# New places for the pieces of a head's step in a gated delta layer, and for a pair of query blocks in sparse attention

## The chip, the cores and the metric

The kernel runs on one core of a Trainium2 chip. The time is the device time of one execution in microseconds (us); a kernel's time is the median of several executions. A profile is one further execution, recorded instruction by instruction.

## The reference, cut to what matters

Two layers over 2048 tokens of width 1024: sparse attention on a shared latent (8 heads, 256 selected keys a query), then a gated delta layer (8 heads of 128, causal convolution, decay, a state carried over the sequence). Each is followed by its output projection and a gated embedding.

```
def sparse_latent_attention(q_lat, q_idx, w_idx, c_kv, k_idx, rel_bias, topk):
    ...
        _, sel = lax.top_k(score, topk)
        ...
        logits = jnp.einsum("bqhc,bqkc->bqhk", qb, c_sel).astype(jnp.float32)
        logits = logits + jnp.moveaxis(bias, -1, 2).astype(jnp.float32)
        logits = jnp.where(valid[:, :, None, :], logits, NEG_INF)
        prob = jax.nn.softmax(logits, axis=-1).astype(c_sel.dtype)
        return jnp.einsum("bqhk,bqkc->bqhc", prob, c_sel)

def chunked_gated_delta_rule(q, k, v, g, beta):
    ...
    lower = jnp.where(strict, jnp.einsum("bhntd,bhnjd->bhntj", kb, kc) * decay, 0.0)
    a_mat = lower + jnp.eye(CHUNK, dtype=jnp.float32)
    rhs = jnp.concatenate([vc * bc[..., None], kb * jnp.exp(gc)[..., None]], axis=-1)
    sol = lax.linalg.triangular_solve(a_mat, rhs, left_side=True, lower=True)
    u_pre, w_dec = sol[..., :dv], sol[..., dv:]
    aqk = jnp.where(incl, jnp.einsum("bhntd,bhnjd->bhntj", qc, kc) * decay, 0.0)
    ...
    def step(state, xs):
        u_p, w_d, a_qk, q_d, k_d, cd = xs
        u = u_p - jnp.einsum("bhck,bhkv->bhcv", w_d, state)
        o = jnp.einsum("bhck,bhkv->bhcv", q_d, state) + jnp.einsum("bhct,bhtv->bhcv", a_qk, u)
        state = state * cd[..., None, None] + jnp.einsum("bhck,bhcv->bhkv", k_d, u)
        return state, o
```

## The kernel before

The program runs in five stages, one after the other: projections, index scores and top-k (`phase1`), attention (`phase2`), the first output projection with its gate (`mix(0)`), the delta layer (`phase4`), and the second output projection (`mix(1)`). Matmuls take f32 values as a high and a low part (three matmuls for one product, `mm3_step`, lines 90 to 92).

Inside a stage several generators run side by side. Each yields a number, its place, ahead of each piece of work, and `weave` always resumes the one with the lowest place. The order in which the pieces are recorded is a priority: a scheduler then orders each engine's instructions by it, with its own estimate of when each is ready, so that an engine's order differs a little from the recorded one. The numbers in the program therefore set what stands behind what on TensorE (PE), VectorE (DVE), ScalarE (ACT), GpSimd (POOL) and in the DMA queue of SyncE (SP). Every engine runs its own list in order.

*Attention.* A piece is a pair of query blocks g (0 to 7) of a head h. `at_logits` computes the pair's logits (`lg`, with penalties added into `pr` by DVE, then Exp on ACT); `at_values` transposes the probabilities (`turn`: `pt`, split by ACT and DVE into `ph` and `pl`) and multiplies them with the values (`mult`: `po`). `cost` gives a pair's length in units, `begin` its place, `DELTA` the lag of values behind logits, `MP` the place of `mult` within a step of `turn`, and `at_loads` places the loads of the next pairs.

*The delta layer.* `phase4` goes through 16 steps j (8 heads for each half of the sequence) and two more at the end. In step j these run side by side:

- `project(j)`: the projections k, q, z, v of head j: 4 x 2 x 24 = 192 matmuls of 128x512 (`pBk`, `pBq`, `pBz`, `pBv`, L1521 to L1523), each result then copied by ACT and convolved by DVE (taps, L1466). The next weights are loaded (L1310) and split by `raw_weights` into `wB`: high part on ACT (L1317), low part on DVE (L1319).
- `within(j-1)`: the inverse of the chunk's triangular matrix: transposes `pkt`, products `pkk`, 16 pairs of product and sum on DVE (`tmp`, `inv`, L1639 and L1642), a round trip of `inv` through DRAM (L1648, L1649), its transposition `Tc` (L1652), and from `LV` on the small matmuls `px`, `pd`, `px_1`, `pd_2` that assemble the inverse `U`.
- `beside(j-1)`: `pqs`, `pkq` and the transposes `pvt`.
- `across(j-2)`: the state through 8 chunks c, one after the other: `pks` (PE) to `y` (DVE, L1749) to `pu` (PE) to `uu` (ACT) to `po` (PE) to `state` (DVE, L1762) to the next `pks`. Chunk c has the place `AC + c * AD`.
- `gated(j-3)`: the output of a finished head: `pot`, and the gate.

At the end `ahead` splits the next stage's weights (`wo`, ACT with DVE or POOL) and begins its first products (`poe`).

Of the kernel before, what the change touches and what calls it, by code (L numbers as in the profile page):

```python
# [27 lines left out]
NC = 8  # L28
# [10 lines left out]
def tile_trunk(ctx: ExitStack, tc: tile.TileContext, a: dict, out: bass.AP):  # L39
# [152 lines left out]
    def enter(sb, xbufs):  # L192

        xs = [load_x(sb, b) for b in range(xbufs - 1)]
        hT = None
        for b in range(4):
            for i in range(2):
                yield i / 8 + b / 4
                if hT is None:

                    n = KD if st1["early"] else 2
                    hT = [T(*(("hT", 2) if st1["early"] else ("c8", 4)), [P, n, 2, SB], f"hT{next(uid)}", F32R)
                          for _ in range(0, KD, n)]
                    st1["hT", sb] = [hT[k // n][:, k % n] for k in range(KD)]
                if i == 0 and b + xbufs - 1 < 4:
                    xs.append(load_x(sb, b + xbufs - 1))
                pt = ps("pp", 4, f"xT{sb}_{b}_{i}")
                for k in range(4):
                    nc.tensor.transpose(pt[:, k * P:(k + 1) * P], xs[b][:, (i * 4 + k) * P:(i * 4 + k + 1) * P], ident)
                ts_ = slice(b * P, (b + 1) * P)  # L210
                m = min(n, 4)
                for k in range(i * 4, i * 4 + 4, m):
                    h = hT[k // n][:, k % n:k % n + m]
                    split(pt[:, (k - i * 4) * P:(k - i * 4 + m) * P].rearrange("p (k n) -> p k n", k=m),
                          h[:, :, 0, ts_], h[:, :, 1, ts_])
# [375 lines left out]
    def phase1():  # L591
        with scope("keys", True) as keys:
# [22 lines left out]
            with scope("scores") as base:  # L615
# [13 lines left out]
                def rest():  # L629

                    work = WORK
                    place, t, done = [(0, 0.0)], 0, 0.0
                    while t < total:
                        t += 1
                        done += 1 - sum(w / (b - a_) for sb, w in work.items() for a_, b in [index_at[sb]] if a_ < t <= b)
                        place.append((t, done))

                    def when(w):
                        w = w / whole * place[-1][1]
                        while place and place[0][1] < w and len(place) > 1:  # L640
                            place.pop(0)
                        return place[0][0]

                    parts = [([gates_z(sb) for sb in range(NSB)], 44), ([proj_q()], WQ),
                             ([proj_k(), *([proj_v1()] if VB else [])], WK)]
                    parts = [parts["zqk".index(c)] for c in RO]
                    whole = sum(len(g) * w for g, w in parts)
                    w0 = 0
                    with scope("rest"):
                        for gens, w in parts:  # L650
                            for g in gens:
                                for f in g:
                                    yield when(w0 + f * w)
                                w0 += w
# [254 lines left out]
    PRL, PRS, AHEAD = 4, 4, 2  # L909
    C0, DELTA = 1.5, 7  # L910

# [12 lines left out]
    def phase2():  # L924
# [155 lines left out]

        cost = [4 * g + 3 + C0 for _, g in order]
        begin = list(itertools.accumulate([0] + cost))
# [33 lines left out]
        def at_loads():  # L1116
# [7 lines left out]
            penalties(range(4, 8))  # L1124
            yield -VS + VL * 0.52
            coming[2]()
# [3 lines left out]
            for n, (h, g) in enumerate(order):  # L1130
                yield begin[max(n - 2, 0)] - 0.02
                if n >= 2:
                    prepare(h, g)
                if n % 8 == 3:
                    coming = fetch(h + 1)
                if n >= 3:
                    f = next(coming, None)
                    if f:
                        f()
# [232 lines left out]

    VT, RA, RB = 0.36, 0.31, 0.0127
    AC, AD, LV = 0, 0.11, 0.75
    FX = 0.02

    def phase4():
# [92 lines left out]
        def project(j):  # L1470
# [12 lines left out]
            for i, name in enumerate("kqzv"):  # L1483
# [7 lines left out]
                for sb in range(2):  # L1491
                    ss_ = slice(sb * SB, (sb + 1) * SB)
                    pp = ps("pa", 2, f"pB{name}{j}_{sb}")
                    for k in range(KD):
# [13 lines left out]
                        if new and sb == 1 and k == 7:  # L1508
                            for _ in e:
                                yield at  # L1510
                        if i == GI and sb == 1 and k == 2:
                            gb = m["gb"] = T("raw", 3, [P, NC, P], f"gb{j}", where=pre)
                            g = gc_d[half]
                            nc.sync.dma_start(gb, bass.AP(g.tensor, g.offset + h * P, [[0, P], [H * P, NC], [1, P]]))
                        if n + 1 < 64 and n % 32 != 31:
                            if sb == 0 and k == 0:
                                made["raw"] = load_weights(n + 1)
                            elif sb == 1 and k == 0:
                                ready[n + 1] = raw_weights(n + 1, made.pop("raw"))
# [16 lines left out]

        def by4(name, mm, sink, at):

            for g in range(2):
                yield at  # L1540
                pp = ps("g", 3, f"{name}_{g}")
# [11 lines left out]
        def within(j):  # L1553
# [41 lines left out]

            yield from by4(f"pkk{j}", prod(kT, kT), l_sink, 0.06)
            if j - 2 in ended:
# [70 lines left out]
            for p in range(2):  # L1668
                e, o = q[2 * p], q[2 * p + 1]
                yield LV + 0.06 + p * 0.02  # L1670
                pd = ps("g", 3, f"pd{j}_{p}")
# [21 lines left out]
        def beside(j):  # L1693

            m = made[j]
            yield 0.12
            kT, qT, vT, kt, nk, dT = (m[x] for x in "k q v kt nk dT".split())
# [32 lines left out]
        def across(j):  # L1730
# [7 lines left out]
            for c in range(NC):  # L1738
                first = half == 0 and c == 0
                t0 = AC + c * AD  # L1740
                y = T("gy", 6, [P, P], f"y{j}_{c}")
# [3 lines left out]
                else:  # L1745
# [6 lines left out]
                    nc.scalar.activation(qs, p1[:, P:2 * P], AF.Copy, scale=eg[:, c, h:h + 1])  # L1752
                yield t0 + 0.035
                p2 = ps("r", 3, f"pu{j}_{c}")
                nc.tensor.matmul(p2[:, 0:P], U[:, c], y, start=True, stop=True)
                uu = T("gy", 6, [P, P], f"uu{j}_{c}")
                last["ACT"] = nc.scalar.activation(uu, p2[:, 0:P], AF.Copy, scale=cj[:, c:c + 1]).ins
                yield t0 + 0.07
                p3 = ps("r", 3, f"po{j}_{c}")
# [39 lines left out]
        def ahead(part):  # L1799

            if part == 0:
                for r in range(8):
                    yield r / 16
                    wout(1, r)
            n = (2, EARLY - 2)[part]
            for x in range(n):
                b = len(early)
                at = 0.5 + x * 0.25 if part == 0 else x / n
                yield at
# [3 lines left out]
                for c in range(2):  # L1813
                    cs = slice(c * 512, (c + 1) * 512)
                    pp = ps("pa", 2, f"poe{b}_{c}")
                    for k in range(KD):
                        t = wo[1][k // 4][:, k % 4, :, cs]
                        mm3_step(pp, y[:, 0, k], y[:, 1, k], t[:, 0], t[:, 1], k == 0, k == KD - 1)
                        if k % 2:
                            yield at + (c * 4 + k // 2 + 1) / 9 * (0.25 if part == 0 else 1 / n)  # L1820
                    nc.vector.tensor_tensor(xt[:, cs], pp, xt[:, cs], ALU.add)
# [6 lines left out]
        for j in range(n + 2):  # L1828
# [12 lines left out]
    F1 = 3  # L1841
    MP = 0.9
    VB = 3
    RO = "zkq"
    WQ = 90
    WK = 42
    VS, VL, V0, V1 = (40, 39.5, 39, 20)
    PLAN = ({3: (0, 120), 2: (120, 260), 1: (300, 400), 0: (430, 470)},
            {3: (122, 300), 2: (302, 415), 1: (417, 480), 0: (482, 530)}, 520)
    pre = ctx.enter_context(tc.tile_pool(name="pre", bufs=1))  # L1850
# [74 lines left out]
```

## Time and profile before

| what | us |
|---|---|
| median of 3 runs | 3472.86 (3471.24 to 3486.31) |
| the profiled execution | 3468.28 |
| its span, first to last instruction | 3466.6 |
| attention in it | about 920 to 1440 |
| delta layer in it | about 1860 to 3110 |

In the rows of the profile `pu L1755 <- DVE y L1749` reads: the instruction on `pu` at line 1755 waited for the one on `y` at line 1749. "x8" counts instructions in a row that is merged; a number in brackets is the time that the engine stood idle before it. The granted clock is TensorE's, 1.00 being full.

### The profile page before, as it was taken

To read this page: it belongs to the slowest core of one execution; us is meant where nothing else is said; L and a number is where in the kernel's file an instruction comes from. 1 tells how busy PE (TensorE), PEld (TensorE's weight loads), DVE (VectorE), ACT (ScalarE), POOL (GpSimd) and SP (SyncE) were. 2 spreads that over 40 slices of the span, in tenths; PEclk is the share of its full clock that TensorE was granted. 3 is DMA by queue.
4 is the path that set the end of the run, shared out by engine and by line. 5 is a ranking of instruction groups with operands and counts; after the bars stand their busy time and mean duration, and the time that the engine had idled before them with its cause. 6 is when DMAs were issued, how large, how long until landed. Compare 5 with 4: busy or idle time off the path is not lost.

```text
span 3466.6 us, 52296 instructions
## 1 busy us (share of the span) xinstructions
PE 3321.1 (96%) x19082; PEld 2786.5 (80%) x19082; DVE 2102.7 (61%) x4566; ACT 1882.7 (54%) x3319; POOL 943.2 (27%) x1620
## 2 busy tenths in 40 slices
PE   8999988988899999999999999999999999899999
PEld 6778777877799999888887788887788888778887
DVE  5367896865588888622225667667667676633222
ACT  5366947675677777543335565555555555433221
POOL 2022435145645444211100221222121222321100
PEclk9999998999899999999999999999999999899999
DMA  6322344442522222422223222213222222233211
GB/s 218 114 77 68 102 148 145 172 152 98 183 78 85 80 85 74 136 95 64 72 64 94 58 50 55 53 45 93 54 58 50 58 51 57 86 130 116 73 34 72
DMA packets 325294, 311.71 MB, mean 90 GB/s; under 512 B 69448, under 2 KB 272808, under 8 KB 322984
## 3 DMA queue, kind: packets, MB, share of 16 engines
q1 hardware_dynamic: 325032, 308.33, 29.8%
q8 instruction: 150, 2.46, 0.3%
q14 instruction: 112, 0.92, 0.1%
HBM read 212.85 MB, written 95.42 MB: 89 GB/s over the span
## 4 chain that ended last, share of the span: by engine, by line
PE 53%; DVE 11%; DMA 4%; ACT 2%; POOL 2%; issue 2%; SPq 0%; DVEq 0%; ACTq 0%; POOLq 0%
PE pgm L91 3%; PE pgm L92 3%; PE pgm L90 3%; PE pt L1024 3%; DVE tmp L1639 3%; PE pom L91 2%; PE pom L90 2%; PE pom L92 2%; PE po L1044 2%; PE po L1045 2%; PE pBv L1521 2%; PE pBv L1522 2%; DVE inv L1642 2%; PE lg L92 2%; PE pBv L1523 2%
## 5 line engine op out<-in xcount | busy, mean ns | idle before, releaser
L79 DVE TENSOR_TENSOR pl<-pt,ph 128x512 fp32r<-128x512 f32 (+1 forms) x288 | 187.5, 657 | 45.8 <-ACT ph L78 43.6
L78 ACT ACTIVATE ph<-pt 128x512 fp32r<-128x512 f32 (+1 forms) x288 | 160.1, 564 | 97.5 <-PE pt L1024 90.3
L1006 ACT ACTIVATE pr<-pr,nm,qscale 128x1024 f32<-128x1024 f32 (+2 forms) x192 | 189.6, 988 | 41.0 <-DVE nm L1003 39.7
L423 DVE SCALAR_TENSOR_TENSOR score<-rl,wi,score 128x1024 f32<-128x1024 f32 (+7 forms) x154 | 169.0, 1119 | 39.6 <-ACT rl L415 38.8
L1247 DVE TENSOR_TENSOR gm<-ppm,gm 128x512 f32<-128x512 f32 x64 | 43.4, 689 | 244.4 <-ACT gm L1246 244.4
L1024 PE MATMUL pt<-ident,pr 128*128 128x128 f32 x1088 | 169.6, 276 | 7.6 <-ACT pr L1006 4.9
L729 DVE TENSOR_SCALAR_CACHE_REDUCE tkj<-score,t 128x1664 bf16<-128x1664 f32 (+3 forms) x91 | 121.7, 1353 | 86.8 <-POOL t L769 79.2
L415 ACT ACTIVATE rl<-il 128x1024 f32<-128x1024 f32 (+7 forms) x176 | 143.2, 819 | 54.8 <-PE il L92 49.2
L90 PE MATMUL pom<-wo,ym 128*128 128x512 f32 x432 | 171.0, 396 | 1.9 <-DVE y L1056 1.1
L91 PE MATMUL pom<-wo,ym 128*128 128x512 f32 x432 | 168.9, 391 | 1.3 <-POOL wo L87 1.3
L91 PE MATMUL pgm<-wm,xh 128*128 128x512 f32 x432 | 168.7, 390 | 1.5 <-DVE wm L82 1.5
L90 PE MATMUL pgm<-wm,xh 128*128 128x512 f32 x432 | 168.8, 391 | 0.6 <-ACT gm L1246 0.6
L92 PE MATMUL pom<-wo,ym 128*128 128x512 f32 x432 | 168.8, 391 | 0.0
L92 PE MATMUL pgm<-wm,xl 128*128 128x512 f32 x432 | 168.7, 390 | 0.0
L1044 PE MATMUL po<-pl,kv 128*128 128x256 f32 x576 | 162.8, 283 | 1.2 <-DVE pl L79 1.2
L1043 PE MATMUL po<-ph,kv 128*128 128x256 f32 x576 | 160.9, 279 | 1.5 <-ACT ph L78 1.5
L1045 PE MATMUL po<-ph,kv 128*128 128x256 f32 x576 | 162.1, 281 | 0.0
L87 POOL TENSOR_TENSOR ym<-yr,ym 128x1024 fp32r<-128x1024 f32 x32 | 77.1, 2409 | 303.5 <-ACT ym L86 303.4
L1246 ACT ACTIVATE gm<-pgm,rm_r 128x512 f32<-128x512 f32 x64 | 42.9, 684 | 183.8 <-PE pgm L91 117.5
L87 POOL TENSOR_TENSOR w<-wr,w 128x512 fp32r<-128x512 f32 x74 | 107.0, 1456 | 130.8 <-ACT w L86 122.8
L1752 ACT ACTIVATE qs<-pks,eg 128x128 f32<-128x128 f32 x120 | 44.0, 367 | 177.5 <-DVE y L1749 171.1
L727 ACT ACTIVATE tkj<-score,t 128x1920 bf16<-128x1920 f32 (+3 forms) x91 | 127.8, 1405 | 23.0 <-POOL t L769 19.8
(636 smaller groups left out, 10908.5 us busy)
## 6 DMA issues: line engine op xcount, KB each, us to landing
wBr<-in_b_w_in_dram SPq DMA_DIRECT2D x64, 512.0 KB
wr<-in_a_w_in_dram SPq DMA_DIRECT2D x74, 256.0 KB
yr<-yT_d SPq DMA_DIRECT2D x32, 512.0 KB
x<-in_x_dram SPq DMA_DIRECT2D x16, 512.0 KB
xn_d<-x SPq DMA_DIRECT2D x16, 512.0 KB
x<-xn_d SPq DMA_DIRECT2D x16, 512.0 KB
zT_d<-z SPq DMA_DIRECT2D x32, 256.0 KB
k_d<-k SPq DMA_DIRECT2D x16, 512.0 KB
```

The source lines that it names most:

```text
L78: nc.scalar.activation(hi, src, AF.Copy)
L79: nc.vector.tensor_tensor(lo, src, f32(hi), ALU.subtract)
L87: nc.gpsimd.tensor_tensor(lo, src, f32(hi), ALU.subtract)
L90: nc.tensor.matmul(dst, ah, bh, start=first, stop=False)
L91: nc.tensor.matmul(dst, ah, bl, start=False, stop=False)
L92: nc.tensor.matmul(dst, al, bh, start=False, stop=last)
L423: nc.vector.scalar_tensor_tensor(sc[:, s0:s1], rl[:, :s1 - s0], w, sc[:, s0:s1], ALU.mult, ALU.add)
L1006: nc.scalar.activation(pr[:, s0:s1], pr[:, s0:s1], AF.Exp, bias=nm, scale=sc, accum_out=den[:, i % 2, x:x + 1])
L1024: nc.tensor.transpose(pt[:, x * P:(x + 1) * P], probs[h, i][:, j * P:(j + 1) * P], ident)
L1043: nc.tensor.matmul(d, V[0][:, j], ph[:, c], start=st, stop=False)
L1044: nc.tensor.matmul(d, V[0][:, j], pl[:, c], start=False, stop=False)
L1045: nc.tensor.matmul(d, V[1][:, j], ph[:, c], start=False, stop=sp)
```

## The change

Numbers only, but for one condition: places of pieces in attention and in the delta layer. Every engine has the same instructions as before, in another order, but for two loads of an activation table on ACT that fall away (each is put where two neighbours need different tables). Phase 1 stays as it was (its lines in the diff are other ways of writing the same numbers). The core of the diff:

```
-    C0, DELTA = 1.5, 7
+    C0, DELTA = 1.269, 8.2959
-        cost = [4 * g + 3 + C0 for _, g in order]
+        cost = [3.7993 * g + 3 + C0 for _, g in order]
-            yield -VS + VL * 0.52
+            yield -VS + VL * 0.6127
-                yield begin[max(n - 2, 0)] - 0.02
+                yield begin[max(n - 2, 0)] - 1.0534
-    MP = 0.9
+    MP = 1.3291
...
-    VT, RA, RB = 0.36, 0.31, 0.0127
-    AC, AD, LV = 0, 0.11, 0.75
-    FX = 0.02
+    VT, RA, RB = 0.3282, 0.31, 0.0127
+    AC, AD, LV = 0.0, 0.11, 0.8179
+    FX = 0.0219
...
-                            if sb == 0 and k == 0:
+                            if (sb, k) == (0, 0):
                                 made["raw"] = load_weights(n + 1)
-                            elif sb == 1 and k == 0:
+                            if (sb, k) == (0, 7):
                                 ready[n + 1] = raw_weights(n + 1, made.pop("raw"))
...
-            yield from by4(f"pkk{j}", prod(kT, kT), l_sink, 0.06)
+            yield from by4(f"pkk{j}", prod(kT, kT), l_sink, 0.06, 0.0105)
-            yield 0.12
+            yield 0.086
-                t0 = AC + c * AD
+                t0 = AC + c * AD - (0.0317 if c == NC - 1 else 0)
-                yield t0 + 0.035
+                yield t0 + 0.0279
-                yield t0 + 0.07
+                yield t0 + 0.0918
-                at = 0.5 + x * 0.25 if part == 0 else x / n
+                at = 0.5842 + x * 0.25 if part == 0 else x / n
```

What that does to the engines' lists is shown at three places. The names are those of the program; in `y_6`, `pks_6`, `po_5` the number behind the name is the chunk c.

DVE in the middle of a head's step (step j = 5), before, from the state of chunk 5 to `y` of chunk 6:

```order
L1762 SCALAR_TENSOR_TENSOR state<-state,cd_23341,po_5_24443 128x128
L1639 TENSOR_TENSOR tmp_24083<-inv_24082,blk_24076 128x392
L1766 TENSOR_TENSOR vt_23564<-po_5_24443,qs_5_24415 128x128
L1642 TENSOR_REDUCE inv_24082<-tmp_24083 128x7x2
L1319 TENSOR_TENSOR wB_24449<-wBr_24386,wB_24449 128x1024
L1639 TENSOR_TENSOR tmp_24083<-inv_24082,blk_24076 128x480
L1749 SCALAR_TENSOR_TENSOR y_6_24448<-pks_6_24466,neg_21234,vt_23564 128x128
```

The same place now:

```order
L1319 TENSOR_TENSOR wB_24436<-wBr_24386,wB_24436 128x1024
L1639 TENSOR_TENSOR tmp_24090<-inv_24089,blk_24083 128x364
L1762 SCALAR_TENSOR_TENSOR state<-state,cd_23341,po_5_24454 128x128
L1642 TENSOR_REDUCE inv_24089<-tmp_24090 128x7x2
L1766 TENSOR_TENSOR vt_23564<-po_5_24454,qs_5_24415 128x128
L1639 TENSOR_TENSOR tmp_24090<-inv_24089,blk_24083 128x392
L1749 SCALAR_TENSOR_TENSOR y_6_24459<-pks_6_24466,neg_21234,vt_23564 128x128
```

The split `wB` has moved from between the state and `y_6` to ahead of the state, and the product 128x480 from before `y_6` to behind it.

TensorE near the end of the same step, before: the small matmuls that assemble the inverse, among the last projection (`pBv_1`), behind 172 of the step's 192 projection matmuls:

```order
L1523 MATMUL pBv_1_24609<-hB_0_20698,wB_24449 128x512
L1521 MATMUL pBv_1_24609<-hB_0_20698,wB_24449 128x512
L1664 MATMUL px_00_24512<-Tc_24481,LT_23991 32x32 x8
L1664 MATMUL px_01_24536<-Tc_24481,LT_23991 32x32 x8
L1522 MATMUL pBv_1_24609<-hB_0_20698,wB_24449 128x512
L1523 MATMUL pBv_1_24609<-hB_0_20698,wB_24449 128x512
L1673 MATMUL pd_0_24558<-Uc_24480,X_0_24511 32x32 x8
L1673 MATMUL pd_1_24583<-Uc_24480,X_0_24511 32x32 x8
```

Now, behind 179 of them:

```order
L1521 MATMUL pBv_1_24583<-hB_0_20698,wB_24436 128x512
L1522 MATMUL pBv_1_24583<-hB_0_20698,wB_24436 128x512
L1664 MATMUL px_00_24542<-Tc_24485,LT_23991 32x32 x8
L1664 MATMUL px_01_24557<-Tc_24485,LT_23991 32x32 x8
L1523 MATMUL pBv_1_24583<-hB_0_20698,wB_24436 128x512
L1521 MATMUL pBv_1_24583<-hB_1_20699,wB_24436 128x512
L1673 MATMUL pd_0_24591<-Uc_24484,X_0_24535 32x32 x8
L1673 MATMUL pd_1_24610<-Uc_24484,X_0_24535 32x32 x8
```

The group has moved seven projection matmuls on. Its last member, `pd_2`, had six projection matmuls behind it in the step and now stands at the start of the next step, right ahead of the transposes `pkt`; `pu_0` of that next step stands six projection matmuls earlier than before.

DVE at the end of the layer, when no projection is left, before: `y` of chunk 1 of the last head but one, and what stands around it:

```order
L1577 TENSOR_SCALAR ncj_31734<-cj_31730 128x8
L1775 SCALAR_TENSOR_TENSOR ss_31706<-ss_31706,sq_30561 128x8
L1749 SCALAR_TENSOR_TENSOR y_1_31800<-pks_1_31809,neg_26493,vt_31283 128x128
L1594 SCALAR_TENSOR_TENSOR LT_31705<-pkk_0_31758,ncj_31734,dT_31737 128x128 x4
L1594 SCALAR_TENSOR_TENSOR LT_31705<-pkk_1_31767,ncj_31734,dT_31737 128x128 x4
L1600 RECIPROCAL rs_31707<-rs_31707 128x8
```

Now:

```order
L1766 TENSOR_TENSOR vt_31283<-po_0_31797,qs_0_31712 128x128
L1594 SCALAR_TENSOR_TENSOR LT_31705<-pkk_0_31758,ncj_31734,dT_31737 128x128 x4
L1594 SCALAR_TENSOR_TENSOR LT_31705<-pkk_1_31771,ncj_31734,dT_31737 128x128 x4
L1775 SCALAR_TENSOR_TENSOR ss_31706<-ss_31706,sq_30561 128x8
L1749 SCALAR_TENSOR_TENSOR y_1_31802<-pks_1_31811,neg_26487,vt_31283 128x128
L79 TENSOR_TENSOR wo_4_31869<-wor_4_31870,wo_4_31869 128x1024
```

The eight products `LT` have moved from behind `y_1` to ahead of it.

More of the change, by code (lines that the diff above doesn't have):

```diff
@@ L197, in enter @@
             for i in range(2):
-                yield i / 8 + b / 4
+                yield (i / 8 + b / 4)
                 if hT is None:
@@ L642, in when @@
                         return place[0][0]
-                    parts = [([gates_z(sb) for sb in range(NSB)], 44), ([proj_q()], WQ),
+                    parts = [([gates_z(sb) for sb in range(NSB)], 44.0), ([proj_q()], WQ),
                              ([proj_k(), *([proj_v1()] if VB else [])], WK)]
@@ L1510, in project @@
                                 yield at
-                        if i == GI and sb == 1 and k == 2:
+                        if i == GI and (sb, k) == (1, 2):
                             gb = m["gb"] = T("raw", 3, [P, NC, P], f"gb{j}", where=pre)
@@ L1535, in ch, with by4 @@
             return slice(c * P, (c + 1) * P)
-        def by4(name, mm, sink, at):
+        def by4(name, mm, sink, at, more=0.0):
             for g in range(2):
-                yield at
+                yield at + g * more
                 pp = ps("g", 3, f"{name}_{g}")
@@ L1669, in within @@
                 e, o = q[2 * p], q[2 * p + 1]
-                yield LV + 0.06 + p * 0.02
+                yield LV + 0.0609 + p * 0.02
                 pd = ps("g", 3, f"pd{j}_{p}")
@@ L1802, in ahead @@
                 for r in range(8):
-                    yield r / 16
+                    yield r * 0.0625
                     wout(1, r)
@@ L1819, in ahead @@
                         if k % 2:
-                            yield at + (c * 4 + k // 2 + 1) / 9 * (0.25 if part == 0 else 1 / n)
+                            yield at + (c * 4 + k // 2 + 1) / 9 * (0.25 if part == 0 else 1.3319 / n)
                     nc.vector.tensor_tensor(xt[:, cs], pp, xt[:, cs], ALU.add)
@@ L1841, in tile_trunk @@
     F1 = 3
-    MP = 0.9
+    MP = 1.3291
     VB = 3
     RO = "zkq"
[L1845 to L1849, printed above, removed]
+    WQ = 90.0
+    WK = 42.0
+    VS, VL, V0, V1 = (40.0, 39.3825, 38.628, 20)
+    PLAN = ({3: (0, 120), 2: (120, 260), 1: (300, 400), 0: (430, 470)}, {3: (122, 300), 2: (302, 415), 1: (417, 480), 0: (482, 530)}, 520)
     pre = ctx.enter_context(tc.tile_pool(name="pre", bufs=1))
```

## The prediction

> **What bounds the kernel now.** I read the page first, then the busy time by stretch, the waits of TensorE, the granted clock in short stretches, and at last single rows in order of time.
>
> ```profile
> span 3466.6 us, 52296 instructions
> PE 3321.1 (96%) x19082; PEld 2786.5 (80%) x19082; DVE 2102.7 (61%) x4566; ACT 1882.7 (54%) x3319; POOL 943.2 (27%) x1620
> ```
>
> TensorE is busy 96% of the span, and no instruction is added or dropped on it. All that new places can win is the 145 us in which it stands still, and time lost to a lowered clock. The next rows show how much of it lies where the change reaches: attention (about 920 to 1440 us) and the delta layer (about 1860 to 3110 us).
>
> ```profile
> 920.00:1440.00 520.00, 515.70 (x3780) 483.14 (x3779) 450.25 (x1423) 380.53 (x711) 239.44 (x288) 1.00 0.28 84
> ...
> 1990.00:2300.00 310.00, 304.83 (x1992) 253.25 (x1991) 218.99 (x502) 176.35 (x338) 71.89 (x163) 0.99 0.23 54
> 2300.00:2520.00 220.00, 205.01 (x1329) 165.93 (x1328) 146.25 (x325) 115.63 (x213) 47.30 (x108) 0.96 0.27 68
> 2520.00:2935.00 415.00, 407.69 (x2737) 339.72 (x2736) 292.26 (x661) 235.98 (x450) 100.35 (x228) 1.00 0.23 54
> 2935.00:3110.00 175.00, 160.79 (x952) 128.87 (x951) 94.70 (x214) 75.39 (x145) 50.62 (x66) 0.91 0.31 94
> ```
>
> The columns are busy time of PE, its weight load, DVE, ACT and POOL, then the clock. Attention has 4.3 us of idle PE in 520 us. The quiet heads of the delta layer (1990 to 2300 and 2520 to 2935) have 5.2 and 7.3 us. The turn between the halves of the sequence (2300 to 2520) has 15.0 us at clock 0.96, the end of the layer 14.2 us at clock 0.91. So the delta layer decides. Its waits on TensorE, from 1860 to 3110 us:
>
> ```profile
> PE pu L1755 <- DVE y L1749: 15.0, 16, 3.4
> ...
> PE pks L1747 <- DVE state L1762: 5.5, 6, 2.5
> PE px L1664 <- DVE Tc L1652: 5.3, 3, 2.5
> ...
> PE pBz L1521 <- ACT wB L1317: 1.4, 2, 0.9
> ```
>
> Then the clock (the third number from the end), in stretches that I cut where it falls:
>
> ```profile
> 1960.00:1965.00 5.00, 5.00 (x36) 3.67 (x33) 1.64 (x2) 1.81 (x3) 0.68 (x2) 0.66 0.06 14
> 2245.00:2250.00 5.00, 5.00 (x45) 3.64 (x43) 1.22 (x3) 1.38 (x3) 0.22 (x2) 0.67 0.51 72
> 2315.00:2325.00 10.00, 10.00 (x98) 7.33 (x93) 3.01 (x5) 2.73 (x6) 1.91 (x5) 0.67 0.33 42
> 2395.00:2405.00 10.00, 8.57 (x60) 8.08 (x60) 7.07 (x12) 6.60 (x13) 2.98 (x9) 0.66 0.32 105
> 2465.00:2470.00 5.00, 4.60 (x14) 3.61 (x14) 3.73 (x6) 0.03 (x1) 0.00 (x0) 0.66 0.81 142
> 2975.00:2990.00 15.00, 15.00 (x121) 11.43 (x119) 6.89 (x8) 7.02 (x12) 4.01 (x4) 0.66 0.21 60
> 2995.00:3025.00 30.00, 23.51 (x108) 19.20 (x108) 16.18 (x38) 15.34 (x27) 19.37 (x19) 0.72 0.43 132
> ```
>
> A stretch of 5 us at 0.66 loses 1.7 us. The first three and the one at 2975 lie just behind the matmuls px of a head; together they lose 1.7 + 1.65 + 3.3 + 5.1 = 11.75 us.
>
> **The change part by part.**
>
> *A. The split of a projection weight (wB, L1319) moves up on DVE, away from y_6.* The stall before:
>
> ```profile
> 2091.86 0.39 PE L1747 MATMUL pks<-state,kT 128*128 128x128 f32 x2
> 2092.08 0.39 PE L1748 MATMUL pks<-state,qT 128*128 128x128 f32 x2
> 2092.20 1.22 DVE L1319 TENSOR_TENSOR wB<-wBr,wB 128x1024 fp32r<-128x1024 f32 x1
> ...
> 2092.77 0.39 PE L1523 MATMUL pBz<-hB,wB 128*128 128x512 f32 x1
> 2093.00 0.39 PE L1521 MATMUL pBz<-hB,wB 128*128 128x512 f32 x1
> ...
> 2093.34 1.00 DVE L1639 TENSOR_TENSOR tmp<-inv,blk 128x480 f32<-128x480 f32 x1
> ...
> 2094.24 0.35 DVE L1749 SCALAR_TENSOR_TENSOR y<-pks,neg,vt 128x128 f32<-128x128 f32 x1
> ...
> 2094.65 0.49 PE L1755 MATMUL pu<-y,U 128*128 128x128 f32 x2 [0.81 <-DVE y L1749]
> ```
>
> pks has ended about 2092.5, but y stands behind the split and one product of the inverse on DVE, and pu waits 0.81 us. The same row over 1925 to 2400 us and over 2530 to 2935 us:
>
> ```profile
> PE pu L1755 <- DVE y L1749: 4.4, 6, 0.8
> ...
> PE pu L1755 <- DVE y L1749: 4.9, 6, 0.8
> ```
>
> So 9.3 of the 15.0 us are twelve such waits in the quiet heads; 5.7 us belong to the turn and the end. In the new order only one product (128x392) stands right before y_6, and the split stands six rows ahead of y_6, between the ones for y_5 and state_5. DVE's work between state_3 and state_6 is no less for it, except that another split, the one behind state_3, goes to before it, where DVE has room: po_3 is issued 15 projection matmuls after pu_3, at 0.23 us each (2092.77 to 2093.00) some 3.5 us. So the 9.3 us can go, but a part returns: pks_5 and pks_7 now follow their po by 4 and 3 projection matmuls, where it was 6. What that costs is bounded by these rows:
>
> ```profile
> 2089.16 0.85 DVE L1639 TENSOR_TENSOR tmp<-inv,blk 128x364 f32<-128x364 f32 x1
> ...
> 2129.11 0.39 PE L1761 MATMUL po<-uu,aq 128*128 128x128 f32 x2
> ...
> 2129.81 0.34 DVE L1762 SCALAR_TENSOR_TENSOR state<-state,cd,po 128x128 f32<-128x128 f32 x1
> ```
>
> The state is there 1.04 us after the second po began; with 3 matmuls between (0.14 + 3 x 0.23 = 0.83 us) pks waits about 0.2 us, with 4 nothing, and up to 0.85 us more where a product of that size has just begun on DVE. Two places in some 14 heads: 3 us at the low end, 27 us at the high end. I take 0.3 us a head, 4.3 us, near the low end, since DVE's order keeps the same count of products ahead of the state. **A is -5 us**, from -9 to +18.
>
> *B. px comes later.* It stood behind 172 of a head's 192 projection matmuls, now behind 179 (the last heads of each half differ by a few).
>
> ```profile
> 2172.87 0.43 DVE L1652 STREAM_TRANSPOSE Tc<-Uc 128x256 f32<-128x256 f32 x1
> ...
> 2173.47 1.09 PE L1664 MATMUL px<-Tc,LT 32*32 32x32 f32 x32
> ...
> 2313.87 0.45 DVE L1652 STREAM_TRANSPOSE Tc<-Uc 128x256 f32<-128x256 f32 x1 [1.33 <-DMA Uc<-iv_d]
> ...
> 2314.46 1.07 PE L1664 MATMUL px<-Tc,LT 32*32 32x32 f32 x32 [1.32 <-DVE Tc L1652]
> ```
>
> In a quiet head px begins 0.17 us after Tc ends: there is no slack, and where the round trip of the inverse through DRAM lands late, px waits (5.3 us in 3 heads, the longest 2.5). Seven matmuls are 1.6 us of slack; of the three waits about 0.9 us is left. Tc now stands behind one convolution tap in DVE's order, which uses that slack up in a quiet head but doesn't add to a late landing. **B is -4.5 us**, from -5.3 to +3 (0.2 us in each of 16 heads).
>
> *C. The clock behind px.* Three of the four low stretches behind px follow a wait of 1.3 us or more. If the wait goes, I expect the low stretch to go as well, two thirds of the 11.75 us: **C is -8 us**, from -12 to +35 (the rival below).
>
> *D. The weights come a step earlier* (new place for the split: the last matmul step of the first half of a chunk). This should end the waits of pBz for wB, 1.4 us, and the low clock behind them at 2465 (1.7 us): **D is -3 us**, from 0 to -7 with the stretch at 2395 (3.4 us).
>
> *E. Attention.* The order of TensorE keeps its cycle of logits, transposes and value products; only the lag of values behind logits grows (values start 8.3 units after their pair's logits, of some 141 units a head; it was 7 of 148). With 4.3 us of idle time in 520 us there is little to win, and four `pr` buffers for the large pairs still suffice, as a pair's last transposes are issued before the second next large pair begins. **E is -1 us**, from -4 to +2.
>
> *F. The end of the layer.* There y_1 of the last but one head moves behind eight products LT.
>
> ```profile
> 2995.80 2.39 DVE L1775 SCALAR_TENSOR_TENSOR ss<-ss,sq 128x8 f32<-128x8 f32 x1
> ...
> 2998.12 0.34 DVE L1749 SCALAR_TENSOR_TENSOR y<-pks,neg,vt 128x128 f32<-128x128 f32 x1
> ...
> 2998.38 2.14 DVE L1594 SCALAR_TENSOR_TENSOR LT<-pkk,ncj,dT 128x128 f32<-128x128 f32 x8
> 2998.51 0.79 PE L1755 MATMUL pu<-y,U 128*128 128x128 f32 x2 [3.41 <-DVE y L1749]
> ```
>
> TensorE has nothing else there, so the eight, 2.14 us, come on top of the 3.41 us. **F is +2 us**, from -6 (what follows starts earlier in the new order) to +6 at half clock. Two loads of an activation table fall away on ACT, 54% busy and not waited for at those places: nothing.
>
> Sum: -5 - 4.5 - 8 - 3 - 1 + 2 = **-19.5 us**. The profiled execution took 3468.28 us, 1.7 us over its span and 4.6 us below the median of the three runs (3472.86). On the median it gives 3453.4, on the profiled execution 3448.8. I take **3453 us**.
>
> **The rivals.**
>
> *R1, the clock doesn't follow the waits.* For it: the stretch at 2245 comes after a wait of px of only 0.12 us. It may be the small matmuls themselves, which stay. Then C is nothing: 3461 us. The Trainium skill, "TensorE: Matmul & The Clock Gate", section "HAM oscillation — how this bites in real kernels", sets the danger at idle gaps of over about 3.4 us; by that rule, too, waits of 1.3 to 2.5 us lower no clock and their end saves none. The trace speaks against the rule as a threshold, since TensorE was busy all of the low stretches at 1960, 2245 and 2315.
>
> *R2, the waits only move.* DVE is the engine that y and state queue on, its work between them stays, and a product of 0.85 us is paid in full at both places of 14 heads, 23.8 us: A is then +15 instead of -5. 3473 us. Against it: before, gaps of 3 matmuls between po_3 and pks_4 caused no wait in the quiet heads.
>
> *R3, slower.* The group px, pd, px_1, pd_2 and the transposes of the next head stand closer together (pd_0 to px_1 has 3 projection matmuls between, where it had 5). If that lowers the clock in every head, twelve heads more pay the mean of the four, 2.9 us each: +35 us, and C is lost: 3496 us. With C lost, -11.5 us are left, so from a fourth such further head on the gain is gone, and with ten the kernel is over 0.5% slower. Against it: the heads from 2520 to 2935 ran at clock 1.00 with the group nearly as dense.
>
> *R4, more is won.* The turn and the end have 29 us of idle time and 0.34 x 10 + 0.28 x 30 = 11.8 us of lost clock; if the earlier weights and the earlier y bring a third of it beside the sum: -14 us, 3439 us.
>
> **How the numbers follow.** The forecast has a chance of 0.45, with 3442 to 3463 as its own range; R1 0.18, R2 0.13, R3 0.06, R4 0.18. The range reaches from below R4 to R2: **3430 to 3476**. A measurement of this kernel can tell about 0.5%, 17.4 us, so faster means below 3455.5: R4 whole (0.18), two thirds of the forecast's range (0.30) and a quarter of R1 (0.05) give **0.53** for faster, **0.40** for the same, **0.07** for slower.
>
> **What would show it.** In the new profile the waits of pu for y in the quiet heads should be gone (A), px without waits over 1 us (B), the clock 1.00 in 1990 to 2300 and behind 2310 (C), pBz without a wait for wB (D), the wait of pu near 3000 us longer than 3.41 us (F). Waits of pks for the state above 8 us in total would be R2. Clocks below 0.7 behind px in more than four heads would be R3. A change of over 5 us in attention would make E wrong.

## The result, and the profile after

The changed kernel takes 3446.89 us, median of 8 runs (3435.66 to 3466.15); the kernel before, run beside it, 3482.96 us (8 runs, 3471.24 to 3487.19). The ratio is **0.9912**, 95% interval 0.9889 to 0.9935: 22 to 39 us less, 31 us at the middle (the two medians lie 36 us apart). The prediction was 3453 us, 19.5 us less. The profiled execution took 3446.69 us.

The head of the page after, then three of the prediction's stretches, the quiet heads and the end of the layer (busy time of PE, its weight load, DVE, ACT and POOL, then the clock):

```profile
span 3444.9 us, 52293 instructions
PE 3314.3 (96%) x19082; PEld 2788.1 (81%) x19082; DVE 2129.6 (62%) x4566; ACT 1877.9 (55%) x3317; POOL 955.6 (28%) x1620
```

```profile
1990.00:2300.00 310.00, 309.18 (x2040) 260.21 (x2039) 231.12 (x514) 179.68 (x345) 78.44 (x165) 1.00 0.23 54
...
2520.00:2935.00 415.00, 413.14 (x2730) 347.00 (x2729) 298.71 (x656) 234.00 (x448) 106.75 (x228) 0.97 0.24 54
2935.00:3110.00 175.00, 160.95 (x969) 129.73 (x969) 95.66 (x196) 66.81 (x128) 50.21 (x63) 0.94 0.37 115
```

The idle time of PE in the quiet heads has fallen from 5.2 and 7.3 us to 0.8 and 1.9 us. The clock has not recovered: 2520 to 2935 ran at 1.00 before and at 0.97 now. The waits of PE from 1860 to 3110 us, and the clock in the stretches where it falls:

```profile
PE pu L1755 <- DVE y L1749: 9.5, 4, 7.4
PE pks L1747 <- DVE state L1762: 5.9, 7, 3.3
PE px L1664 <- DVE Tc L1652: 3.9, 11, 1.0
...
PE pot L1547 <- POOL vt L1790: 1.4, 2, 0.9
...
PE pBz L1523 <- DVE wB L1319: 0.9, 1, 0.9
...
PE pBz L1521 <- ACT wB L1317: 0.5, 1, 0.5
```

```profile
2375.00:2385.00 10.00, 10.00 (x55) 8.27 (x54) 2.79 (x5) 4.52 (x9) 1.17 (x4) 0.51 0.29 105
2455.00:2465.00 10.00, 7.61 (x24) 6.33 (x25) 5.09 (x9) 5.31 (x8) 0.23 (x1) 0.66 0.48 118
2615.00:2625.00 10.00, 10.00 (x66) 7.96 (x66) 1.36 (x3) 2.61 (x5) 0.19 (x1) 0.56 0.19 17
2750.00:2770.00 20.00, 19.94 (x158) 15.80 (x157) 8.62 (x18) 9.55 (x18) 5.37 (x13) 0.66 0.16 24
```

px waits eleven times now, 1.0 us at the longest (it was three times, up to 2.5 us); the view lists no wait below 0.15 us. The stretches behind px have moved to other heads (2615, 2750).

A head's step is measured here from its first projection matmul to that of the next head. Head 4, before and after:

```profile
2115.63 0.47 PE L1521 MATMUL pBk<-hB,wB 128*128 128x512 f32 x1
...
2184.61 0.48 PE L1521 MATMUL pBk<-hB,wB 128*128 128x512 f32 x1
```

```profile
2109.69 0.47 PE L1521 MATMUL pBk<-hB,wB 128*128 128x512 f32 x1
...
2176.87 0.47 PE L1521 MATMUL pBk<-hB,wB 128*128 128x512 f32 x1
```

68.98 us have become 67.18, and heads 3 to 6 of the changed kernel agree within 0.03 us; so **1.8 us a quiet head** can be taken apart by single profiles. The span fell by 21.7 us: the twelve quiet heads (2 to 6 and 9 to 15) -21.8, heads 0 and 1 -5.4, the turn (heads 7 and 8) +2.7, the end of the layer +2.1, all other stages +0.6. The runs fell by more, since the profiled execution of before, at 3468.28 us, is below all eight runs of before that stood beside the changed kernel.

A source of the gain that the prediction does not have is in the rows of POOL. In the waits of before (1860 to 3110 us) it stands second:

```profile
PE pot L1547 <- POOL vt L1790: 5.8, 13, 1.0
...
PE pBz L1521 <- ACT qT L1530: 1.9, 2, 1.6
```

(The second row is for term D below.) Before, in head 4, and below it the changed kernel:

```profile
2120.72 2.16 DVE L1594 SCALAR_TENSOR_TENSOR LT<-pkk,ncj,dT 128x128 f32<-128x128 f32 x8
...
2122.79 0.19 DVE L1600 RECIPROCAL rs<-rs 128x8 f32<-128x8 f32 x1
2123.08 4.20 POOL L1790 TENSOR_SCALAR vt<-vt,rs 128x128 f32<-128x128 f32 x8 [1.78 <-DVE rs L1600]
2125.75 0.82 PE L1547 MATMUL pot<-ident,vt 128*128 128x128 f32 x6
...
2126.98 0.68 PE L1547 MATMUL pot<-ident,vt 128*128 128x128 f32 x2 [0.41 <-POOL vt L1790]
2127.41 0.48 PE L1521 MATMUL pBk<-hB,wB 128*128 128x512 f32 x1
```

```profile
2114.50 1.13 DVE L1594 SCALAR_TENSOR_TENSOR LT<-pkk,ncj,dT 128x128 f32<-128x128 f32 x4
...
2115.85 0.20 DVE L1600 RECIPROCAL rs<-rs 128x8 f32<-128x8 f32 x1 [0.22 <-ACT rs L1599]
2116.14 1.13 DVE L1594 SCALAR_TENSOR_TENSOR LT<-pkk,ncj,dT 128x128 f32<-128x128 f32 x4
2116.14 4.19 POOL L1790 TENSOR_SCALAR vt<-vt,rs 128x128 f32<-128x128 f32 x8 [2.20 <-DVE rs L1600]
...
2119.81 1.04 PE L1547 MATMUL pot<-ident,vt 128*128 128x128 f32 x8
2120.61 0.47 PE L1521 MATMUL pBk<-hB,wB 128*128 128x512 f32 x1
```

The second half of pkk is put 0.0105 of a step later, and so DVE makes `rs` between the two groups of four LT instead of behind all eight. POOL scales `vt` from there on, 3.7 us before pot instead of 2.7, and pot no longer catches up with POOL. From the first pot to the next projection matmul it took 1.66 us (2125.75 to 2127.41) and takes 0.80 now: twice what the wait of 0.41 us shows, since the matmuls on either side of it were further apart as well.

### The profile page after: what moved, and what is told of

Its sections match the earlier page's. It is cut to its first block, busy times and chain, and to the rows that moved or that the text cites. A ratio compares the mean times of both kernels' runs of the same rounds, so it can differ in the third digit from the quotient of the medians.

```text
span 3444.9 us, 52293 instructions
## 1 busy us (share of the span) xinstructions
PE 3314.3 (96%) x19082; PEld 2788.1 (81%) x19082; DVE 2129.6 (62%) x4566; ACT 1877.9 (55%) x3317; POOL 955.6 (28%) x1620
## 4 chain that ended last, share of the span: by engine, by line
PE 61%; DVE 4%; DMA 4%; ACT 3%; issue 2%; POOL 1%; SPq 0%; ACTq 0%; POOLq 0%; DVEq 0%
PE pgm L91 3%; PE pgm L90 3%; PE pgm L92 3%; PE pt L1024 3%; PE pom L90 2%; PE pom L92 2%; PE pom L91 2%; PE pBk L1521 2%; PE pBk L1523 2%; PE pBk L1522 2%; PE po L1044 2%; PE po L1045 2%; PE pBv L1521 2%; PE lg L92 2%; PE pBv L1523 2%
## 5 line engine op out<-in xcount | busy, mean ns | idle before, releaser
L1639 DVE TENSOR_TENSOR tmp<-inv,blk 128x4 f32<-128x4 f32 (+15 forms) x256 | 137.2, 536 | 4.4
```

## The experiments

Two theories on a quiet head were set against each other: A, the prediction's (the wB split stood ahead of y_6), and P (`rs` stood behind LT). X is that the denser recurrence itself saves time, J that the edits only act together, S that each has its own price. W, L and the random draw are about the low clock: by W a px that waits, however little, lets it fall, by L the later place of px does, with or without a wait, and by the random draw neither matters.

**One edit at a time, from the kernel before.** The pkk edit alone:

```
-            yield from by4(f"pkk{j}", prod(kT, kT), l_sink, 0.06)
+            yield from by4(f"pkk{j}", prod(kT, kT), l_sink, 0.06, 0.0105)
```

> Only the second half of the pkk step is put 0.0105 later; everything else stands as before. On DVE the reciprocal rs then stands between the two groups of four LT products in the quiet heads, and no wB split moves. Theory A (the prediction's step A: what a quiet head gains is the pu wait behind the wB split): nothing is gained, a quiet head stays at 68.98 us within 0.2, and pot waits for vt as before (0.41 us a head). Theory P (rs earlier starts the scaling on POOL earlier, and pot no longer waits for it): the pot wait goes, the eight pot matmuls take about 0.9 us less a head, and a quiet head takes 68.1 us.

The split's place alone:

```
-                            elif sb == 1 and k == 0:
+                            elif sb == 0 and k == 7:
```

> Only the wB splits of the next pair of heads' weights are put at (sb, k) = (0, 7) instead of (1, 0); rs stays behind all eight LT products. Theory A: the pu wait for y_6 (0.8 us a quiet head) goes and a quiet head takes 68.2 us, with pot's wait of 0.41 still there. Theory P alone: 68.98 us stays, since what the splits delayed comes back as another wait. If both hold, this run and the one with the pkk half moved add up to most of the 1.8 us.

The places of pu, po and the last chunk alone:

```
-                t0 = AC + c * AD
+                t0 = AC + c * AD - (0.0317 if c == NC - 1 else 0)
-                yield t0 + 0.035
+                yield t0 + 0.0279
-                yield t0 + 0.07
+                yield t0 + 0.0918
```

> Only the places of pu, po and the last chunk in the recurrence are changed; px stays behind 172 projection matmuls. Theories A and P both give 68.98 us for a quiet head, within 0.3. A third theory X (the denser spacing of pks, pu and po itself saves PE time: pu fell by 0.26 and po by 0.15 us a head in the changed kernel) gives 68.6 us.

And all edits but the attention's (six times; the three above have a single time each, 3465.6 to 3479.2 us, which decides nothing):

> All edits of the delta layer, none of the attention. If the delta layer makes the whole gain (the attention's stages stood within 0.9 us in the two profiles): a quiet head at 67.15 us within 0.1, and a ratio of 0.991 as with the whole change. If the attention's new places had made 5 us or more of it: a ratio of 0.993 or above. On step C: if the half-clock stretches behind px follow the waits, they stand at the heads of the changed kernel's profile (near 2380, 2460, 2620, 2760 us); if they are drawn anew in each execution, at other heads.

The waits of PE from 1990 to 2300 us, first the pkk edit, then the split's place, then pu and po (before, they are 3.3 us of pu in four heads and 1.7 of pot):

```profile
PE pu L1755 <- DVE y L1749: 3.3, 4, 0.8
```

```profile
PE pu L1755 <- DVE y L1749: 2.5, 4, 0.7
PE pot L1547 <- POOL vt L1790: 1.8, 4, 0.5
PE po L1760 <- ACT uu L1757: 1.3, 5, 0.3
```

```profile
PE pot L1547 <- POOL vt L1790: 1.7, 4, 0.4
PE pks L1747 <- DVE state L1762: 1.4, 5, 0.3
```

The quiet head took 68.23 us with the pkk edit, 69.54 with the split's place and 68.90 with pu and po. P holds: pot's wait is gone, for 0.75 us. A falls as stated: the split's place alone leaves 0.6 of the 0.8 us of pu's wait, adds waits of po and makes the head 0.57 us **longer**. Of the three only the spread of pu and po takes pu's wait away, and alone it pays with waits of pks. X falls (0.07 us). The three come to -0.25 us of the 1.8. The delta layer alone had 67.19 us and 0.9928 (0.9903 to 0.9954), so the gain is its own. Its clock fell behind px in heads 3, 6, 10, 13 and 14, where the changed kernel's, with the same edits of this layer, fell in 10 and 12: the low stretches are drawn anew in each execution.

**One edit left out of the delta layer's, attention as before:** the split's place, the pkk edit, pvt with the inversion (VT) and the products beside, and pu with po.

> All edits of the delta layer but one: the wB splits stay at (1, 0). On DVE a quiet head's y_6 then stands one place behind a wB split, the state and the vt rows and ahead of tmp of 480, instead of three places further from the split. Theory J (the edits act jointly: alone the splits' place cost 0.57 us a quiet head, 69.54 against 68.97, but with the other edits it clears y_6): without it 0.6 to 0.8 us of pu wait come back and a quiet head takes 67.8 to 68.0 us. Theory S (each edit has its own price): 67.15 - 0.57 = 66.6 us.

> All edits of the delta layer but one: the second half of pkk stays beside the first, so that rs stands behind all eight LT products. Theory P: pot's wait for vt is back, and the quiet head takes 0.75 us more than 67.15, 67.9 us (the edit alone took 0.75 us off). If the other edits had already cleared pot: 67.15 us.

> All edits of the delta layer but one: pvt and with it the inversion's chain stay at 0.36, and the key and query products beside them at 0.12. px then stands behind 172 projection matmuls again. By the prediction's step B this costs px waits of about 1 us in some heads and nothing else: 67.2 to 67.6 us a quiet head. By theory J the earlier chain is what brings tmp of 392 ahead of y_6 without a wait: pu waits of 0.8 us come back, 68.0 us.

> All edits of the delta layer but one: pu, po and the last chunk keep their places in the recurrence. Alone this edit took the pu wait of 0.83 us a head away and put three pks waits of 0.14 to 0.3 us in its place (68.9 against 68.97). Theory J: without it the pu wait for y_6 or another of about 0.8 us is back, 67.9 to 68.0 us. Theory S: 67.15 + 0.07 = 67.2 us.

The waits from 1990 to 2300 us without the split's place, without pkk, without VT, and without pu and po (rows of px, 0.6, 0.7 and 0.7 us in all but the third, are left out; the single times are 3465.1, 3461.9, 3443.1 and 3470.4 us):

```profile
PE pks L1747 <- DVE state L1762: 1.3, 4, 0.3
```

```profile
PE pot L1547 <- POOL vt L1790: 1.4, 3, 0.5
```

```profile
PE pks L1747 <- DVE state L1762: 2.3, 5, 0.5
```

```profile
PE pot L1547 <- POOL vt L1790: 1.6, 4, 0.4
PE po L1760 <- ACT uu L1757: 1.2, 5, 0.2
```

| left out | quiet head, us | against 67.15 |
|---|---|---|
| split's place | 67.53 | +0.4 |
| pkk | 68.47 | +1.3 |
| VT and beside | 67.93 | +0.8 |
| pu and po | 68.58 | +1.4 |

S falls: the four come to 3.9 us, twice the gain. J holds in that the edits act together, but not by the waits that it named: pu's wait came back in none of the four (no row above has it), not even without pu and po, so y_6 does not hang on the split nor on any one of them, and the expectation of pu waits was wrong three times. By the rows, VT and the split's place take back the waits of pks that pu and po make alone, and pot stays clear only with pkk and with pu and po. The rows show only a part of each cost (0.6 of the 1.4 us without pu and po); the rest is not taken apart here.

**What lowers the clock behind px.** The trace's clock changes only on a grid of 3413 ns, which starts elsewhere in each execution. The changed kernel at 2615 us, cut on that grid (the clock is the third number from the end):

```profile
2610.15:2613.56 3.41, 2.48 (x63) 2.11 (x64) 2.70 (x5) 0.85 (x3) 2.05 (x4) 1.00 0.28 67
2613.56:2616.97 3.41, 3.41 (x29) 2.49 (x26) 0.42 (x1) 1.27 (x3) 0.00 (x0) 0.50 0.93 68
...
2623.80:2627.21 3.41, 3.41 (x26) 3.08 (x25) 3.13 (x5) 3.04 (x6) 0.20 (x1) 1.00 0.00 0
...
2750.10:2753.51 3.41, 3.35 (x70) 2.56 (x68) 2.48 (x5) 1.38 (x4) 1.86 (x4) 1.00 0.48 67
2753.51:2756.92 3.41, 3.41 (x24) 2.08 (x23) 0.42 (x1) 0.76 (x2) 0.00 (x0) 0.50 0.46 71
```

The first step holds px with its wait, 0.98 us here, the longest of the quiet heads; the three behind it run at half clock although PE is busy throughout. At 2750 us the step with px has 0.06 us of idle time, and the clock falls behind it too. The Trainium skill, "TensorE: Matmul & The Clock Gate", section "What's actually happening", has a free-running window of 3413 ns; the trace agrees.

Why px waits in every head now is plain in DVE's rows of head 4, changed kernel:

```profile
2165.18 0.68 ACT L1530 ACTIVATE vT<-pBv,b_conv_w 128x512 f32<-128x512 f32 x1
2165.97 0.95 DVE L1466 SCALAR_TENSOR_TENSOR vT<-xbv,b_conv_w,vT 128x512 f32<-128x512 f32 x1 [0.95 <-POOL xbk L1528]
2166.84 0.43 DVE L1652 STREAM_TRANSPOSE Tc<-Uc 128x256 f32<-128x256 f32 x1
...
2167.42 1.07 PE L1664 MATMUL px<-Tc,LT 32*32 32x32 f32 x32 [0.28 <-DVE Tc L1652]
```

A convolution tap stands ahead of Tc now, and it starts behind ACT's `vT` (2165.18 + 0.68 = 2165.86), which comes from PE's own projection; the view names the small copy of `xbk` on POOL, which ends 0.1 us later. So the later px is followed by a later Tc.

Four kernels were made from the changed one. Tc made twice, and (with VT and the products beside as before) px at 172 without a wait, and there Tc made three times:

```
+                for _ in range(2):
                     nc.vector.transpose(Tc.rearrange("p c t -> p (c t)"), Uc.rearrange("p c t -> p (c t)"))
```

```
-    VT, RA, RB = 0.3282, 0.31, 0.0127
+    VT, RA, RB = 0.36, 0.31, 0.0127
...
-            yield 0.086
+            yield 0.12
```

> The changed kernel, with the transpose that makes Tc done twice (0.43 us more on DVE in each head, the same result). px then stands behind 183 instead of 179 projection matmuls (0.94 us later), so that it no longer waits for Tc. In the ten profiles so far, half-clock stretches of 1.7 us or more behind px began in 12 or 13 of the 48 quiet heads (numbers 2 to 6 and 9 to 15) of the four kernels whose px waits 0.06 to 0.7 us in every head, and in 1 of 47 heads whose px does not wait. Theory W (a px that waits, however little, is what lets the clock fall): at most 1 of the 12 quiet heads has a stretch, a quiet head takes 66.9 to 67.3 us, and the ratio to the kernel before is 0.988 (about 12 us below the changed kernel's time). Theory L (px at a later place lets it fall, with or without a wait): 3 of 12 heads, and the changed kernel's time, 0.991.

> The changed kernel with its attention, but pvt and the inversion's start at 0.36 and the products beside at 0.12 as before: px behind 172 matmuls, without a wait, three pks waits (0.56 us a head) instead. Theories W and L both: at most 1 of 12 quiet heads with a half-clock stretch, a quiet head at 67.93 us; 0.78 us x 12 heads are lost against the changed kernel and its stretches (some 10 to 15 us) won, so a ratio of 0.990. If stretches come at random: 3 of 12, and 0.993.

> The kernel with pvt at 0.36 again, with the transpose that makes Tc done three times (0.87 us more on DVE in each head, the same result). px stands behind 179 instead of 172 matmuls and, coming 1.65 us later for 0.87 us more, does not wait. Theory W: at most 1 of 12 quiet heads has a half-clock stretch. Theory L: about 3 of 12, as with the other kernels that have px behind 179. A quiet head takes 67.9 to 68.2 us by both.

And the changed kernel with the taps kept behind Tc:

```
+                last["Tc"] = nc.vector.transpose(Tc.rearrange("p c t -> p (c t)"), Uc.rearrange("p c t -> p (c t)")).ins
...
+                with behind("Tc"):
                     nc.vector.scalar_tensor_tensor(y, xb[:, t:t + SB], w[:, t:t + 1], y, ALU.mult, ALU.add)
```

> The changed kernel with one order forced: DVE's convolution rows of v may not stand ahead of the transpose that makes Tc. In the changed kernel the first of them does, right behind the wB split, and it waits for ScalarE's copy of the projection that PE has just done; Tc ends 0.15 us ahead of px there, and px waits 0.06 to 0.3 us in each quiet head. With Tc right behind the split, px (now behind 176 instead of 179 matmuls) finds it done about 1 us before. Theory W (a px that waits lets the clock fall): no px wait, at most 1 of the 12 quiet heads with a half-clock stretch, a quiet head at 66.9 us, and 10 to 18 us below the changed kernel, a ratio to the kernel before of 0.986 to 0.988. Theory L (it is the later place, not the wait; px at 176 is nearer to the 179 than to the 172 of the kernels without stretches): about 3 of 12 heads, and 0.990 to 0.991.

| kernel | ratio to before (95%) | mean clock of its runs |
|---|---|---|
| before | 1 | 0.979 (17, run beside Tc twice and VT as before) |
| changed | 0.9912 (0.9889 to 0.9935) | 0.978 (8) |
| Tc twice | 1.0005 (0.9988 to 1.0022) | 0.974 (12) |
| VT as before | 0.9902 (0.9882 to 0.9921) | 0.984 (6) |
| taps behind Tc | 0.9921 (0.9899 to 0.9943) | 0.979 (6) |

The quiet heads of the kernel with Tc twice, then of the one with VT as before (clock third from the end):

```profile
1990.00:2300.00 310.00, 305.01 (x1939) 251.35 (x1939) 215.20 (x492) 172.42 (x330) 79.68 (x161) 0.97 0.22 52
2520.00:2935.00 415.00, 412.56 (x2692) 347.54 (x2691) 294.37 (x658) 232.15 (x444) 105.99 (x224) 0.95 0.21 51
```

```profile
1990.00:2300.00 310.00, 307.22 (x2017) 255.74 (x2016) 232.61 (x511) 179.17 (x343) 74.31 (x164) 1.00 0.23 56
2520.00:2935.00 415.00, 411.67 (x2761) 343.06 (x2760) 308.59 (x671) 241.14 (x463) 103.96 (x231) 1.00 0.23 56
```

Making Tc twice did not end px's waits: the second transpose ended up behind another tap, px waits up to 0.6 us, pot waits again, the half clock takes 29 us from the quiet heads (12 us in the changed kernel), and **0.43 us more on DVE a head cost the whole gain**. With VT as before px did not wait in any quiet head (in two in the run above with the same delta layer), no quiet head has a stretch in either profile, and each is 0.78 us slower for its pks waits; the mean clock is higher (0.984), the heads are longer, and the ratio can't be told from the changed kernel's. Tc three times (a single time, 3457.0 us) left waits of 0.06 us or a little more and three heads with a stretch. Keeping the taps behind Tc missed: px moved up to 176 matmuls, Tc there waited for its DMA (0.96 us in head 4), and three heads had stretches, two of them behind a px that waited 0.04 and 0.07 us. L's number, about three of twelve heads, came out in all three (four, three and three); but px still waited in those heads, so they do not tell L from W. No kernel here beats the changed one by more than the measurement tells.

Counted over the 14 profiles, 168 quiet heads: of 96 in which px waited 40 ns or more, the clock fell within four steps of the grid in 32; of 72 in which it did not, in 1. Where px began less than 900 ns behind a step of the grid, so that its first 64 small matmuls lay in one step, it fell in 15 of 19 with a wait and in 0 of 28 without. With px at 172 (170 to 172) in all, it is 6 of 11 against 1 of 61, so it is not the place alone. L is left open in part: of the late px only 11 did not wait (none fell, one of them in the first 900 ns), and of the px at 172 only one with a wait below 0.5 us began there (it did not fall). A late px that never waits was not tried.

The wait is not the whole of it either: where the grid cuts the group counts as much. Of the 73 px that waited 0.04 to 0.5 us, 12 of 16 fell in the first 900 ns behind a step, 8 of 8 from 2640 to 2800 ns behind one, and none of 49 anywhere else. The one px that fell without a wait began in the second stretch as well (at 2737 ns), so there W is not shown. Of the 23 longer waits, 12 fell, 8 of them outside both stretches. Both stretches were found in the heads that they are counted on, and no run tested them; since the grid starts elsewhere in each execution, which heads are hit is chance.

## Why the prediction came out as it did

The direction and the range held, and the forecast is 6 us above the median. That it is so near is in part luck: the kernel before ran 10 us slower beside the changed one than it did ahead of the prediction, and as a difference 19.5 us was forecast and 31 (22 to 39) measured. Several of its steps were wrong in ways that partly cancel: a gain of the clock that did not come stands against a gain at pot that was left out. Its ceiling, "the 145 us in which it stands still" and the lowered clock, was too narrow as well: by the two profiles idle time of PE fell by 14.9 us, but busy time by 6.8 (3321.1 to 3314.3), as at pot, where a wait also spreads the matmuls around it. Measured in the two profiles:

- **A** (-5). The waits of pu in the twelve quiet heads went, 9.9 us, and the 0.3 us a head of new pks waits did not come there. The size was too small and the cause wrong: "moves up on DVE, away from y_6" was credited to the split, which alone lengthens the head. The pks waits appear in the turn (3.8 us in head 8, before none).
- **Left out.** pot's wait for POOL stood second in the view of waits that the prediction quoted, 5.8 us in 13 (the row shown above), and was passed over; the edit that ends it was not costed at all. It is worth 0.75 us a head alone and 1.3 together, 9 to 16 us over twelve heads: the largest term of the sum was missing.
- **B** (-4.5). px waits fell from 5.6 to 4.1 us over the layer, -1.5. The three long ones went, but behind the tap px waits 0.06 to 0.28 us in eleven quiet heads, which stood in B's upper bound, and 0.98 us in the twelfth.
- **C** (-8). The step that failed. The time lost to the clock in the quiet heads went from 10.2 to 12.0 us (half of the time at half clock); over the runs the mean clock is the same. That a fall follows a waiting px was nearly always so (32 of 33); that shorter waits would mean fewer falls was wrong, since a fall has followed 0.04 us, and where the grid cuts the group counts as much as the wait. The time is R1's for C; its reason, the small matmuls themselves, is not borne out alone (1 fall in 72 heads without a wait), but has a part in where the falls come.
- **D** (-3). pBz's waits fell from 3.7 to 1.5 us over all heads, -2.2, but not by the step: the waits for wB, which were to end, went from 1.8 us to 1.4 (the rows above), and the wait for ACT's `qT`, 1.9 us, is what went. The half clock there (2455) came again and lasted 6.8 us instead of 3.4. The size is luck.
- **E** (-1). Attention took 556.5 us before and 557.4 after, from the first `lg` to the last `po`. In nine profiles with the old places it took 556.5 to 561.2 us, in five with the new ones 557.2 to 558.2: about -2 us, within its bounds; the profile of before was the fastest of its kind.
- **F** (+2). From the last projection matmul to the first of the output projection it took 28.9 us, now 31.1: +2.1. The wait grew, as said, but by 4.0 us (3.41 to 7.44), not by the 2.14 of the eight products; PE's other waits in that stretch shrank by 2.3, so the sum is right and its terms are not:

```profile
2978.64 2.14 DVE L1594 SCALAR_TENSOR_TENSOR LT<-pkk,ncj,dT 128x128 f32<-128x128 f32 x8
...
2980.78 0.34 DVE L1749 SCALAR_TENSOR_TENSOR y<-pks,neg,vt 128x128 f32<-128x128 f32 x1
...
2981.17 0.79 PE L1755 MATMUL pu<-y,U 128*128 128x128 f32 x2 [7.44 <-DVE y L1749]
```

R2 did not come: pks waits 5.9 us in all, below its mark of 8. R3 did not come in this kernel (two quiet heads with a fall), though the kernel with Tc twice, with four, came nearest to it. The time lies between the forecast and R4, but not where R4 put it: the turn got 2.7 us longer.

## What to carry to other kernels

Cost every wait that a view of waits lists, above all one that is short and comes in every round: 0.4 us behind POOL in every head was worth 9 to 16 us in all. Time that a wait costs is not only its own row: price an edit by the whole step, from one iteration's start to the next. In a kernel whose orders are interlocked, do not credit a gain to the edit that stands nearest to the wait: taken alone, the split's place lost time. Where small matmuls wait for another engine, give that engine's result a clear lead, since a wait of 0.04 to 0.3 us was followed by half a clock for 3 to 14 us in 18 of the heads counted here; and do not price a change by the low stretches of one profile, since they are drawn anew in each execution.

## What was not expected of the hardware

The clock falls with PE busy and after waits far below one step of its grid. The Trainium skill, "TensorE: Matmul & The Clock Gate", section "HAM oscillation — how this bites in real kernels", gives idle gaps of over about 3.4 us as the danger. Here the clock fell behind px's group of 32x32 matmuls in 12 of 16 heads in which its first 64 lay within one step of 3413 ns with a wait of 0.04 to 0.34 us, and in none of 28 without a wait; the measurement decides. Whether it is the group's small tiles that make it so sensitive was not tried.
